# Reordering the seven products of a fast matrix multiply and giving one more of them a second level

## The chip, the cores and the metric

The kernel runs on one core of one Trainium2 chip. The metric is the device time of that core in microseconds (us), as a median over executions. A profiled execution is described by its span, from the first to the last instruction, which lies some 2 us below the time of the same run.

The engines are called as in the profile: PE is TensorE (matmul), DVE is VectorE, ACT is ScalarE, POOL is GpSimd. Each has a queue of instructions of its own.

## The reference

```python
x:  (8, 1024, 1024)   w1: (1024, 4096)   w2: (4096, 1024)      # all float32

h = x @ w1
h = 0.5 * h * (1 + np.tanh(np.sqrt(2 / np.pi) * (h + 0.044715 * h ** 3)))
return (h @ w2).astype(np.float32)
```

## The kernel before

The kernel works in fp16 with fp32 accumulation, in eight *superblocks* of 1024 rows, numbered 0 to 7. Both matmuls use a scheme of the Strassen-Winograd kind: each matrix is cut into 2 x 2 blocks, and seven products M1 to M7 of sums of blocks replace eight. Superblocks 0 and 1 use a separate routine, which also prepares and stores the sums of `w2`. The change is about `matmul2`, the second matmul of superblocks 2 to 7.

Each product multiplies a sum of blocks of the left matrix by a sum of blocks of the right one:

```python
A_TERMS = {1: ("11", "22"), 2: ("21", "22"), 3: ("11", None), 4: ("22", None),
           5: ("12", "11"), 6: ("21", "11"), 7: ("12", "22")}     # left: first minus second
INNER = (6, 7)                     # products of matmul2 that use a second level
ORDER = (4, 5, 1, 2, 3, 7, 6)      # order of the inner products
```

A *plain* product is four row blocks, each 16 matmuls of 512 columns (64 in all). DVE makes the left operand `gc` of a row block by one subtraction. A *two-level* product applies the same scheme again: seven *inner products* of 16 matmuls of 256 columns, 112 in all. DVE first makes four *inner differences* (`inner_x`), then for five of the seven inner products an *inner sum* of two of them:

```python
    def inner_x(m, g):                       # four DVE subtractions, g -> x[b]
        ...
            tt(x[b], g[u][at], g[v][at], SUB)

    def inner_product(m, x, acc, done=lambda b, t: None):
        ...                                  # seven loads of prepared sums of w2
        def product(j, bank, first):
            u, v = A_TERMS[j]
            if v is None:
                t = x[u]                     # inner products 4 and 3: no sum
            else:
                t = gcp.tile([P, HK, HT // 2], GT, name="gc")
                tt(t, x[u], x[v], SUB)       # the inner sum
            ...                              # 16 matmuls
        pb, qb, rb = psum(), psum(), psum()
        product(4, pb, True)
        v = temp()
        nc.scalar.copy(out=v, in_=pb)
        product(5, qb, True)
        u = temp()
        tt(u, v, qb, SUB)
        nc.gpsimd.tensor_tensor(out=part("11"), in0=part("11"), in1=pair(u), op=ADD)
        product(1, rb, True)
        s = temp()
        tt(s, u, rb, ADD)
        product(2, pb, False)
        s2 = temp()
        tt(s2, s, pb, SUB)
        nc.gpsimd.tensor_tensor(out=part("22"), in0=part("22"), in1=pair(s2), op=ADD)
        add("21", pb)                        # tt(part, part, bank, ADD) on DVE
        product(3, qb, False); add("12", qb)
        product(7, rb, False); add("11", rb)
        product(6, qb, False); add("22", qb)
```

The second matmul runs M4, M5, M2, M6, M3, M1, M7. Note where `x6` is made: after M4, before the loop over M5.

```python
    def matmul2(sb, g):
        ...
        for q, ps in product(4, pb, True):
            v[q] = temp()
            nc.scalar.copy(out=v[q], in_=ps)
        u2, u = halves()
        x6 = inner_x(6, g)
        for q, ps in product(5, qb, True):
            tt(u[q], v[q], ps, SUB)
        d2, d = halves()
        for q, ps in product(2, pb, False):
            ...
            tt(d[q], u[q], ps, SUB)
        inner_product(6, x6, d2)
        x7 = inner_x(7, g)
        for q, ps in product(3, qb, False):
            ...
            tt(d[q], d[q], ps, ADD)
        for q, ps in product(1, rb, True):
            tt(u[q], u[q], ps, ADD)
            tt(d[q], d[q], ps, ADD)
            store(sb, "22", q, d[q])
        ...
        inner_product(7, x7, u2)
```

`product` yields row blocks. PE's work for block q is emitted, then the body of the loop runs for it. A scheduler places the instructions of each engine; those emitted with a pin keep their order.

## Time and profile before

| | us |
|---|---|
| median of 3 runs (lowest, highest) | 1561.78 (1561.55, 1562.36) |
| profiled span | 1559.7 |
| PE busy | 1546.6 (99%) |
| mean granted PE clock | 0.998 |
| a plain product of the second matmul (64 matmuls of 512) | 13.82 |
| a two-level product, M7 (112 matmuls of 256) | 12.23 |
| the two-level product M6 | 12.52 |

Two lines of the kernel's page, the busy time of each engine and the share of each in the chain that ended last:

```profile
PE 1546.6 (99%) x7838; PEld 767.8 (49%) x7838; DVE 1004.2 (64%) x1268; ACT 473.1 (30%) x794; POOL 201.0 (13%) x292
PE 93%; DMA 3%; DVE 2%; issue 1%; SPq 1%; POOL 0%; ACT 0%; DVEq 0%
```

The kernel is bound by PE. The waits of PE (what waited, for whom, us in total, times, longest) say the same: four entries, 4.1 us in all, none in the second matmul.

```profile
PE ps L303 <- DVE u L116: 1.5, 1, 1.5
PE ps L239 <- DVE warm L719: 1.2, 1, 1.2
...
```

The timeline of PE before, superblock 4. The columns are start, duration (both us), line, output and inputs, shapes, count; a bracket at the end, where there is one, is the idle time in front and what ended it. Durations contain the pipeline's tail (the first line lasts 1.91 us, and the next starts 1.75 us after it), so products are measured from start to start.

```profile
927.67 1.91 PE L588 MATMUL ps<-u 128*128 128x256 f16 x16
929.42 5.40 PE L588 MATMUL ps<-u,gc 128*128 128x256 f16 x48
934.66 1.91 PE L588 MATMUL ps<-u 128*128 128x256 f16 x16
936.41 3.95 PE L588 MATMUL ps<-u,gc 128*128 128x256 f16 x32
940.20 13.98 PE L644 MATMUL ps<-u,g 128*128 128x512 f16 x64
954.01 13.98 PE L644 MATMUL ps<-u,gc 128*128 128x512 f16 x64
967.82 1.91 PE L588 MATMUL ps<-u 128*128 128x256 f16 x16
```

M6 is the first four lines, 927.67 to 940.20 = 12.53 us. M3 follows, then plain M1, 954.01 to 967.82 = 13.81 us. The fourth line takes 3.95 us where M7's takes 3.66: M6 loses 0.30 us there, too little for PE's waits to list.

The timeline of DVE before shows why M6 is nearly free of stalls: its four inner differences (`u<-g,g`, 4.62 us for all four) run at 887.04, beside M4, some 40 us before M6 needs them.

```profile
887.04 4.62 DVE L116 TENSOR_TENSOR u<-g,g 128x2048 f16<-128x2048 f16 x4
891.58 4.62 DVE L116 TENSOR_TENSOR gc<-g,g 128x2048 f16<-128x2048 f16 x4
```

### The profile page before, as it was taken

To read this page: it belongs to the slowest core of one execution; us is meant where nothing else is said; L and a number is where in the kernel's file an instruction comes from. 1 tells how busy PE (TensorE), PEld (TensorE's weight loads), DVE (VectorE), ACT (ScalarE), POOL (GpSimd) and SP (SyncE) were. 2 spreads that over 40 slices of the span, in tenths; PEclk is the share of its full clock that TensorE was granted. 3 is DMA by queue.
4 is the path that set the end of the run, shared out by engine and by line. 5 is a ranking of instruction groups with operands and counts; after the bars stand their busy time and mean duration, and the time that the engine had idled before them with its cause. 6 is when DMAs were issued, how large, how long until landed. Compare 5 with 4: busy or idle time off the path is not lost.

```text
span 1559.7 us, 20433 instructions
## 1 busy us (share of the span) xinstructions
PE 1546.6 (99%) x7838; PEld 767.8 (49%) x7838; DVE 1004.2 (64%) x1268; ACT 473.1 (30%) x794; POOL 201.0 (13%) x292
## 2 busy tenths in 40 slices
PE   9999999999999999999999999999999999999997
PEld 4444444444444455444554455544554445544454
DVE  6876867758755576564765647556575556655574
ACT  6644024400244103441034410343004430044210
POOL 2241012113200012000120011200111001200011
PEclk9999999999999999999999999999999999999999
DMA  9999876875984469644695446954569455663362
GB/s 317 357 324 340 252 257 221 265 231 177 342 270 132 164 251 322 194 165 149 244 355 153 186 162 239 363 147 162 186 242 334 135 189 206 235 234 135 149 237 74
DMA packets 165954, 354.73 MB, mean 227 GB/s; under 512 B 72800, under 2 KB 79968, under 8 KB 164960
## 3 DMA queue, kind: packets, MB, share of 16 engines
q1 hardware_dynamic: 147456, 282.11, 52.3%
q0 software_dynamic: 18400, 71.32, 13.9%
q8 instruction: 61, 1.00, 0.3%
q14 instruction: 37, 0.30, 0.1%
HBM read 278.92 MB, written 89.13 MB: 236 GB/s over the span
## 4 chain that ended last, share of the span: by engine, by line
PE 93%; DMA 3%; DVE 2%; issue 1%; SPq 1%; POOL 0%; ACT 0%; DVEq 0%
PE ps L303 48%; PE ps L644 39%; PE ps L588 6%; DMA gc<-in_w_dram 1%; DMA u<-w_d 1%; DVE u L116 1%; SPq L126 1%; DVE tmp L116 0%; DMA u<-in_x_dram 0%; DVE gc L116 0%; POOL u L129 0%; ACT u L153 0%; DVEq L116 0%
## 5 line engine op out<-in xcount | busy, mean ns | idle before, releaser
L303 PE MATMUL ps<-u 128*128 128x512 f16 x3584 | 776.0, 379 | 2.9 <-DVE u L116 1.5
L116 DVE TENSOR_TENSOR tmp<-tmp,ps 128x512 f32<-128x512 f32 x564 | 386.3, 686 | 309.0 <-ACT tmp L363 112.9
L303 PEld LDWEIGHTS <-u 128*128 128x128 f16 x3584 | 350.6, 98 | 426.2 <-issue 3.7
L644 PE MATMUL ps<-u,gc 128*128 128x512 f16 x1792 | 389.4, 379 | 0.0
L644 PEld LDWEIGHTS <-gc 128*128 128x128 f16 x1792 | 175.3, 98 | 211.5
L313 ACT ACTIVATE g<-tmp 128x512 f16<-128x512 f32 x256 | 161.2, 630 | 293.9 <-DVE tmp L116 293.8
L644 PE MATMUL ps<-u,g 128*128 128x512 f16 x1024 | 223.6, 379 | 0.0
L313 ACT ACTIVATE g<-ps 128x512 f16<-128x512 f32 x256 | 151.5, 596 | 90.1 <-PE ps L303 90.1
L116 DVE TENSOR_TENSOR u<-u 128x2048 f16<-128x2048 f16 (+2 forms) x154 | 159.5, 1066 | 16.1 <-ACT u L265 12.0
L397 POOL DMA_DIRECT2D out_dram<-tmp x72 | 39.5, 548 | 943.2 <-ACT tmp L688 765.1
L116 DVE TENSOR_TENSOR u<-u,ps 128x512 f32<-128x512 f32 x160 | 106.7, 682 | 83.9 <-ACT tmp L695 37.1
L644 PEld LDWEIGHTS <-g 128*128 128x128 f16 x1024 | 100.3, 98 | 119.5
L116 DVE TENSOR_TENSOR gc<-g,g 128x2048 f16<-128x2048 f16 x112 | 133.1, 1216 | 2.3 <-PE ps L644 1.6
L588 PE MATMUL ps<-u,gc 128*128 128x256 f16 x960 | 109.7, 273 | 0.8
L588 PEld LDWEIGHTS <-gc 128*128 128x128 f16 x960 | 93.9, 98 | 12.7 <-issue 1.9
L363 ACT COPY tmp<-ps 128x512 f32<-128x512 f32 x128 | 72.8, 569 | 86.5 <-PE ps L303 86.4
L116 DVE TENSOR_TENSOR gc<-u 128x2048 f16<-128x2048 f16 x60 | 73.2, 1220 | 39.2 <-PE ps L644 39.2
L116 DVE TENSOR_TENSOR tmp<-ps,tmp 128x512 f32<-128x512 f32 x128 | 88.3, 690 | 6.1 <-PE ps L303 1.2
L116 DVE TENSOR_TENSOR u<-tmp,ps 128x512 f32<-128x512 f32 x24 | 16.5, 688 | 74.7 <-PE ps L644 65.0
L688 ACT COPY tmp<-ps 128x512 f32<-128x512 f32 x24 | 14.1, 586 | 152.0 <-PE ps L644 152.0
L116 DVE TENSOR_TENSOR u<-g,g 128x2048 f16<-128x2048 f16 x48 | 59.9, 1289 | 0.0
L695 ACT COPY tmp<-ps 128x512 f32<-128x512 f32 x24 | 14.0, 585 | 133.5 <-PE ps L644 132.8
(34 smaller groups left out, 359.6 us busy)
## 6 DMA issues: line engine op xcount, KB each, us to landing
u<-w_d SPq DMA_DIRECT2D x192, 512.0 KB, 8.0
u<-raw_d SPq DMA_DIRECT2D x128, 512.0 KB, 7.3
u<-in_d SPq DMA_DIRECT2D x84, 512.0 KB, 8.7
gc<-in_w_dram SPq DMA_DIRECT2D x48, 512.0 KB, 6.0
out_dram<-tmp POOLq DMA_DIRECT2D x72, 256.0 KB, 3.2
raw_d<-u SPq DMA_DIRECT2D x32, 512.0 KB, 9.5
w_d<-u POOLq DMA_DIRECT2D x32, 512.0 KB, 4.0
xb<-in_x_dram POOLq DMA_DIRECT2D x56, 256.0 KB, 11.8
```

Of the source, the lines that this page charges most:

```text
L116: i = nc.vector.tensor_tensor(out=out, in0=in0, in1=in1, op=op)
L126: return tc.keep_in_program_order(nc.sync.dma_start(out=out, in_=in_, **kw))
L303: nc.tensor.matmul(bank, lhsT=ops[m][:, k, cs], rhs=xs[m][:, k, :], start=(first and k == 0), stop=(k == KH - 1), skip_group_check=not first,)
L313: gelu_last[0] = nc.scalar.activation(out=g[b][:, c, :], in_=src, func=GELU)
L363: nc.scalar.copy(out=v, in_=pb)
L397: return nc.gpsimd.dma_start(out=out2[r0:r0 + P, o0:o0 + OH], in_=src)
L588: nc.tensor.matmul(bank[:, i * HO:(i + 1) * HO], lhsT=t[:, c, i * P:(i + 1) * P], rhs=y[j][:, c, :], start=(first and i == 0 and c == 0), ...
L644: nc.tensor.matmul(bank, lhsT=a[:, c, :], rhs=pieces[c // QC][:, c % QC, :], start=(first and c == 0), stop=(c == NI - 1), skip_group_chec ...
L688: nc.scalar.copy(out=c21, in_=ps)
L695: nc.scalar.copy(out=c12, in_=ps)
```

## The change

The intent is to give M1 a second level in superblocks 3 to 7 (less PE work), and to free buffers for it: M1 and M4 are added into `u` first, so M4's copies no longer live in temporaries, the sums `d` come from `u` once M5 is done, and the next `x` blocks load later. The products run as M4, M1, M2, M5, M6, M3, M7. Superblock 2 keeps M1 plain and, beside it, makes and stores the sums of `w2` that a two-level M1 needs. The core of the diff, cut:

```diff
-INNER = (6, 7)
+INNER = (6, 7, 1)
...
+        p4 = product(4, pb, True)
         u2, u = halves()
-        x6 = inner_x(6, g)
+        for q, ps in p4:
+            nc.scalar.copy(out=u[q], in_=ps)
+        if sb == 2:
+            pieces = load(1)
+            for q, ps in product2(g, 1, pieces, rb, True):
+                tt(u[q], u[q], ps, ADD)
+            for j in SUMS + PLAIN:
+                split_inner(1, j, pieces)
+        else:
+            inner_product(1, inner_x(1, g), u2)
+        for q, ps in product(2, pb, False):
+            c21[q] = temp()
+            nc.scalar.copy(out=c21[q], in_=ps)
+            store(sb, "21", q, c21[q])
+        d2, d = halves()
+        xs = next_x()
         for q, ps in product(5, qb, True):
-            tt(u[q], v[q], ps, SUB)
...
-        inner_product(6, x6, d2)
-        x7 = inner_x(7, g)
+            tt(u[q], u[q], ps, SUB)
+            tt(d[q], u[q], c21[q], SUB)
+        inner_product(6, inner_x(6, g), d2)
         for q, ps in product(3, qb, False):
...
-        for q, ps in product(1, rb, True):
-            tt(u[q], u[q], ps, ADD)
-            tt(d[q], d[q], ps, ADD)
             store(sb, "22", q, d[q])
+        x7 = inner_x(7, g)
```

(The next `x` blocks are now transposed by `next_x()`, called before M5; before, they were transposed ahead of the whole second matmul.)

## The prediction

> **What bounds the kernel now.** TensorE. The page gives PE 1546.6 us of 1559.7 (99%), and the waits list of PE holds 4.1 us, all in the first 45 us. The chain of waits is 93% PE. So only matmul columns and new PE stalls can move the time.

> **What the change removes.** The PE timeline gives 13.82 us for a plain product of the second matmul (64 matmuls of 512 columns, 215.9 ns each) and 12.22 us for a two-level one (112 of 256, 109.1 ns each). [...] M1 becomes two-level in superblocks 3 to 7: 5 x 1.60 = 8.0 us less PE work. Superblock 2 keeps plain M1 and pays ten 1024-wide DVE sums (0.74 us each) and 3.7 MB of stores to prepare it; DVE has idle time there, so I count nothing.

> **What it adds and moves.** Each M1 adds four inner differences (1.29 us), five inner sums (1.22 us) and 1.7 MB more loads. Beside M4 DVE has 8 us idle, and the x transposes (16 x 1.26 us on the load queue) fall in M4 and M1, 15 us ahead of M5's loads. I see no stall at M1, M2, M3 or M7.

> **The step I expect to hurt: M6.** Before, M6's four inner differences stood in DVE's queue beside M4, long ahead. In the changed program's order they stand in M5: two after M5's third row block, then the update of u for the *fourth* block (which waits for M5's last matmul), then the third difference, the update of d, the fourth difference, and only then the sum that M6's second inner product (5) needs.  Counted from the end of M5 with the trace's start-to-start times: 0.2 (wait) + 0.6 + 1.14 + 0.6 + 1.14 + 1.22 (the sum itself) = about 5.0 us, against 1.75 us of inner product 4. PE then idles about 3.25 us, in all six superblocks 2 to 7 (the order is the same in each): 19.5 us. Before, M6 lost only 0.30 us (12.52 against 12.22), which vanishes into it: net +17.7 us.

> **Sum (an estimate from these durations):** 1561.8 - 8.0 + 17.7 = 1571.5 us, 0.6% slower. Range for 8 of 10: 1565 to 1579. Chances: faster by over 2% 0.01, within 2% 0.96, slower by over 2% 0.03.

> **What would show it.** In the PE timeline: M1 of superblocks 3 to 7 takes 12.2 to 12.5 us; M6 takes 15 to 16 us, with one gap of 3 to 3.5 us in front of its second inner product; PE's waits list names DVE (the inner sum) some 6 times, 18 to 20 us in total; all other products are unchanged. PE busy time falls by about 8 us while the span grows.

> **What would make it wrong.**
> - [...]
> - If the fourth update did not stand in the way, the time would be 1554.
> - M1 may repeat the 0.3 us stall of the old M6 (+1.5 us).

## The result, and the profile after

| | before | after |
|---|---|---|
| median, us, of the same rounds | 1562.07 (1561.55 to 1562.65, 4 runs) | 1583.15 (1582.05 to 1583.92, 4 runs) |
| profiled span, us | 1559.7 | 1580.8 |
| mean granted PE clock | 0.998 | 0.993 |

The ratio is 1.0134 (95% interval 1.0117 to 1.0152). Here and below, a ratio is the mean time of one kernel's fast runs over that of the other's of the same rounds, so it is not quite the ratio of the medians quoted. The kernel became 1.3% slower, about 21 us. The prediction was 10 us slower, and its range ended at 1579. All four runs of the changed kernel have the clock at 0.993.

The page after, the same two lines as before:

```profile
PE 1548.5 (98%) x8078; PEld 796.1 (50%) x8078; DVE 1039.1 (66%) x1294; ACT 476.2 (30%) x799; POOL 224.9 (14%) x311
PE 88%; DVE 5%; SPq 3%; DMA 2%; issue 1%; ACT 0%; DVEq 0%
```

PE has less work but is busy 1.9 us *longer*. That is the first sign that some matmuls ran slowly. The waits of PE after have two new entries, both at the two-level products:

```profile
PE ps L588 <- DVE gc L116: 19.4, 6, 3.2
PE ps L588 <- DVE u L116: 4.4, 5, 0.9
...
```

The timeline of PE after, superblock 4: two-level M1 in the first five lines, M2 and M5 in the sixth, M6 in the next four, then M3.

```profile
908.92 1.91 PE L588 MATMUL ps<-u 128*128 128x256 f16 x16
910.67 5.40 PE L588 MATMUL ps<-u,gc 128*128 128x256 f16 x48
915.91 1.91 PE L588 MATMUL ps<-u 128*128 128x256 f16 x16
917.66 1.91 PE L588 MATMUL ps<-u,gc 128*128 128x256 f16 x16
920.46 1.91 PE L588 MATMUL ps<-u,gc 128*128 128x256 f16 x16 [0.89 <-DVE u L116]
922.20 27.79 PE L644 MATMUL ps<-u,gc 128*128 128x512 f16 x128
949.83 1.91 PE L588 MATMUL ps<-u 128*128 128x256 f16 x16
954.98 6.92 PE L588 MATMUL ps<-u,gc 128*128 128x256 f16 x48 [3.24 <-DVE gc L116]
961.73 1.91 PE L588 MATMUL ps<-u 128*128 128x256 f16 x16
963.47 3.66 PE L588 MATMUL ps<-u,gc 128*128 128x256 f16 x32
966.97 13.98 PE L644 MATMUL ps<-u,g 128*128 128x512 f16 x64
```

Three things are to be read here.

1. M6 has the predicted gap before its second inner product: 3.24 us are listed, 3.25 were predicted. The two are not quite the same quantity: the prediction counted from start to start, and that delay is 954.98 - 951.58 = 3.40, since a listed idle time begins only when the pipeline has emptied (PE is still busy for 0.16 us after 951.58, in the windows below).
2. The 48 matmuls after the gap take 6.92 us. The same 48 take 5.40 in M1 above and in the kernel before. M6 as a whole lasts 966.97 - 949.83 = 17.14 us, not the 15 to 16 of the prediction.
3. M1 has a gap of its own, 0.89 listed (920.46 - 919.40 = 1.06 in truth), before its last inner product. It lasts 922.20 - 908.92 = 13.28 us, not 12.2.

The queue of DVE after, around the gap of M6. M5 ends and M6 begins on PE at 949.83; its second inner product starts after the first of the four `gc<-u` sums.

```profile
947.96 2.35 DVE L116 TENSOR_TENSOR u<-g,g 128x2048 f16<-128x2048 f16 x2
950.23 0.68 DVE L116 TENSOR_TENSOR u<-u,ps 128x512 f32<-128x512 f32 x1
950.83 1.22 DVE L116 TENSOR_TENSOR u<-g,g 128x2048 f16<-128x2048 f16 x1
951.96 0.68 DVE L116 TENSOR_TENSOR u<-u,tmp 128x512 f32<-128x512 f32 x1
952.57 1.22 DVE L116 TENSOR_TENSOR u<-g,g 128x2048 f16<-128x2048 f16 x1
953.70 4.62 DVE L116 TENSOR_TENSOR gc<-u 128x2048 f16<-128x2048 f16 x4
```

The second line is the update of `u` for M5's fourth row block. It needs M5's last matmul, and two of the four inner differences stand behind it in the same queue. This is word for word the sequence that the prediction had counted: the first sum is ready at 953.70 + 1.22 = 954.92, 5.1 us after M5's end (predicted: about 5.0; the update begins 0.40 us after M5's end and not 0.2; no idle time is listed in front of it, as the two differences ahead of it last until then).

Windows of the same place. Columns: stretch, its length, then for PE, PEld, DVE, ACT and POOL the busy time and (count), then the granted PE clock, the DMA share and GB/s.

```profile
951.58:954.98 3.40, 0.16 (x3) 0.01 (x1) 3.40 (x5) 0.58 (x1) 0.00 (x0) 0.96 0.00 0
954.98:958.08 3.10, 3.10 (x15) 2.23 (x16) 3.10 (x3) 0.00 (x0) 0.00 (x0) 0.50 0.00 0
960.00:962.00 2.00, 2.00 (x21) 1.79 (x19) 1.00 (x3) 0.00 (x0) 1.46 (x1) 1.00 0.93 352
```

The clock drops to 0.50 just before the gap ends (0.96 as the gap's mean puts the drop 0.3 us before its end) and PE then runs 3.1 us at half speed. That costs half of it, about 1.55 us, in each of the six superblocks (from the durations above, 6.92 - 5.40 = 1.52). Read in finer steps, the clock is at 0.50 from 954.68 to 958.09; such a stretch of 3.41 us is called a window from here on.

### Where the 21.1 us of the spans went

| part | predicted | measured | how measured |
|---|---|---|---|
| M6, gap | +17.7 | +18.6 | 15.62 (M6 with its gap at whole clock: 17.14 less 6.92 - 5.40) - 12.52, times 6 |
| M6, half clock | 0 | +9.1 | 102.89 (sum of the six M6 after) - 75.15 (before) - 18.6 |
| M1, superblocks 3 to 7 | -8.0 | -2.7 | (13.28 - 13.82) x 5 |
| end of the kernel, after the last product | 0 | -4.0 | 4.1 after, 8.1 before |
| start | 0 | +0.05 | the difference up to the second matmul of superblock 2 |
| sum | +9.7 | +21.1 | |

The end of the kernel is the surprise of this table. The last product ends at 1551.58 before and at 1576.72 after (start of M7 plus 12.23), and the spans end at 1559.7 and 1580.8. Between the two lies the closing work of the engines. The largest piece is the longest of POOL's three closing DRAINs, shown here before and then after (minimum / median / maximum in ns, then the first and last start):

```profile
L760 POOLq DRAIN  x3: 46/102/11681, 1547.3 to 1559.5; - x3
```

```profile
L769 POOLq DRAIN  x3: 46/102/2867, 1572.4 to 1580.5; - x3
```

The long one begins beside POOL's last addition, at 1547.3 before and 1572.4 after. Before it takes 11.68 us and ends at 1559.0, where POOL's first closing semaphore event also stands, just ahead of the span's end. After it takes 2.87 us and is over before the last product is. Nothing in the diff is meant to touch it.

### The profile page after: what moved, and what is told of

Read it like the earlier page. It is cut to its first block, busy times and chain, and to the rows that moved or that the text cites. A ratio compares the mean times of both kernels' runs of the same rounds, so it can differ in the third digit from the quotient of the medians.

```text
span 1580.8 us, 21061 instructions
## 1 busy us (share of the span) xinstructions
PE 1548.5 (98%) x8078; PEld 796.1 (50%) x8078; DVE 1039.1 (66%) x1294; ACT 476.2 (30%) x799; POOL 224.9 (14%) x311
## 4 chain that ended last, share of the span: by engine, by line
PE 88%; DVE 5%; SPq 3%; DMA 2%; issue 1%; ACT 0%; DVEq 0%
PE ps L303 47%; PE ps L644 31%; PE ps L588 10%; DVE u L116 3%; SPq L288 3%; DMA gc<-in_w_dram 1%; DVE gc L116 1%; DMA u<-in_d 1%; DVE tmp L116 1%; DMA u<-xb 1%; SPq L126 0%; ACT u L191 0%; ACT g L313 0%; SPq L577 0%; ACT u L265 0%
## 5 line engine op out<-in xcount | busy, mean ns | idle before, releaser
L644 PE MATMUL ps<-u,gc 128*128 128x512 f16 x1472 | 319.3, 379 | 0.0
L644 PEld LDWEIGHTS <-gc 128*128 128x128 f16 x1472 | 144.1, 98 | 172.6
L588 PE MATMUL ps<-u,gc 128*128 128x256 f16 x1360 | 163.9, 282 | 23.9 <-DVE gc L116 19.4
L588 PEld LDWEIGHTS <-gc 128*128 128x128 f16 x1360 | 137.1, 101 | 46.1 <-DVE gc L116 21.1
L116 DVE TENSOR_TENSOR u<-u,ps 128x512 f32<-128x512 f32 x136 | 92.6, 684 | 99.6 <-PE ps L644 52.9
L116 DVE TENSOR_TENSOR gc<-g,g 128x2048 f16<-128x2048 f16 x92 | 117.7, 1286 | 52.5 <-PE ps L644 51.1
L611 POOL TENSOR_TENSOR u<-u,tmp 128x512 f32<-128x512 f32 x17 | 37.0, 2174 | 671.2 <-DVE tmp L116 649.4
L116 DVE TENSOR_TENSOR gc<-u 128x2048 f16<-128x2048 f16 x85 | 99.8, 1219 | 0.0
L363 ACT COPY tmp<-ps 128x512 f32<-128x512 f32 x128 | 72.9, 569 | 86.7 <-PE ps L303 86.6
L116 DVE TENSOR_TENSOR u<-g,g 128x2048 f16<-128x2048 f16 x68 | 80.7, 1219 | 3.5 <-ACT g L313 3.5
L588 PE MATMUL ps<-u 128*128 128x256 f16 x544 | 64.9, 273 | 0.0
L704 ACT COPY tmp<-ps 128x512 f32<-128x512 f32 x24 | 14.1, 586 | 160.9 <-PE ps L644 160.9
## 6 DMA issues: line engine op xcount, KB each, us to landing
xb<-in_x_dram POOLq DMA_DIRECT2D x56, 256.0 KB, 11.7
```

The lines of the kernel that those rows point to most:

```text
L116: i = nc.vector.tensor_tensor(out=out, in0=in0, in1=in1, op=op)
L588: nc.tensor.matmul(bank[:, i * HO:(i + 1) * HO], lhsT=t[:, c, i * P:(i + 1) * P], rhs=y[j][:, c, :], start=(first and i == 0 and c == 0), ...
L644: nc.tensor.matmul(bank, lhsT=a[:, c, :], rhs=pieces[c // QC][:, c % QC, :], start=(first and c == 0), stop=(c == NI - 1), skip_group_chec ...
L704: nc.scalar.copy(out=c12, in_=ps)
```

## The experiments

Four theories were to be tested, each with a rival. (a) The gap of M6 comes from where the inner differences are emitted, not from M1's second level. (b) The slow matmuls after it come from the clock, which falls because of the idle time; the rival is that something else slows them, and a second question is how long a gap it takes. (c) M1's gap comes from POOL's two additions; the rivals are the number and order of DVE's operations, and the later `x` loads. (d) The shorter end comes from something that the change altered by accident. The runs came in four calls, each on one chip with the kernel before beside it (its medians 1562.07, 1562.63, 1562.27 and 1562.69), so kernels of different calls are compared through their ratios.

### e1: the inner differences of M6 made before M5's loop

Against the changed kernel:

```diff
-        for q, ps in product(5, qb, True):
+        p5 = product(5, qb, True)
+        x6 = inner_x(6, g)
+        for q, ps in p5:
...
-        inner_product(6, inner_x(6, g), d2)
+        inner_product(6, x6, d2)
```

> The changed kernel with one line moved: M6's four inner differences are made before the loop that updates u and d from M5, so in DVE's queue they stand ahead of the update that waits for M5's last matmul. Theory (queue order): the 3.24 us gap in M6 is gone in all six superblocks, with it the half clock after it; M6 takes 12.2 to 12.5 us instead of 17.1, mean clock back to 0.998, time 1583.2 - 6 x 4.7 = about 1555 us. M1's gap of 0.89 us stays. Rival (late loads: the x blocks moved to M5 or the inner operands come too late): the gap stays, about 1583 us.

Measured: 1554.07 us (1553.27 to 1554.18, 4 runs, results correct), ratio 0.9945 (0.993 to 0.996), clock 1.0. The timeline of PE at M6, superblock 4, e1:

```profile
939.76 1.91 PE L588 MATMUL ps<-u 128*128 128x256 f16 x16
941.51 5.40 PE L588 MATMUL ps<-u,gc 128*128 128x256 f16 x48
```

There is no gap, and the 48 matmuls are back at 5.40. M6 takes 12.23 us. So 29 of 1583 us hang on the position of one call. The span is 1551.2, 8.5 below the kernel before, and the same table accounts for it: M6 -0.3 x 6 = -1.8 (the old small stall is gone), M1 -2.7, the end -4.0. M1's gap of 0.89 is still there.

### e4: the new order alone, M1 plain in every superblock

Against the changed kernel:

```diff
-INNER = (6, 7, 1)
+INNER = (6, 7)
...
-        if sb == 2:
+        if True:
...
-            for j in SUMS + PLAIN:
-                split_inner(1, j, pieces)
```

> The new order of products alone, M1 one-level in every superblock, nothing stored for it. Theory: the loss is in the order, not in M1: M6 keeps its gap of 3.24 us and the half clock, 17 us in all six superblocks, M1 takes 13.8 us without a gap; 1562.6 + 27.9 = 1590 us if the end of the kernel stays as before, 1586 us if the shorter end seen after the change comes from the order. Rival (M1's second level crowds out the rest): M6 back to 12.5 us and the time near 1562.

Measured: 1592.07 us (one run, correct, state unknown), span 1590.3, clock 0.990. M6's gap is there without any second level in M1, 3.25 us in each of six places. With e1 this settles theory (a): the loss comes with the reordering, since the gap is there without M1's second level (e4), but within the new order it hangs on where M6's inner differences are emitted, since moving that one call removes it (e1).

It is 9.5 us of span slower than the changed kernel. Of these, 2.7 us are M1 (plain again) and 4.0 the end (the closing DRAIN is back at 11.687 us). The rest, 2.8 us, is nearly all clock: in two of the six places it stays at half for two windows instead of one, and the 48 matmuls take 8.13 and 8.29 us. One of them in the timeline of PE, e4:

```profile
1152.19 8.29 PE L588 MATMUL ps<-u,gc 128*128 128x256 f16 x48 [3.25 <-DVE gc L116]
```

### e2, e2b and e2c: the gap of M6 filled with matmuls of zeros

The gap keeps its cause, but PE is kept busy for a part of it by matmuls on a tile of zeros into a bank of its own. Only the clock should notice. Against the changed kernel; e2 uses 14 matmuls, e2b 4, e2c 7:

```diff
-    def inner_product(m, x, acc, done=lambda b, t: None):
+    def inner_product(m, x, acc, done=lambda b, t: None, fill=0):
...
         product(4, pb, True)
+        if fill:
+            keep_clock(psum(), fill)
...
-        inner_product(6, inner_x(6, g), d2)
+        inner_product(6, inner_x(6, g), d2, fill=14)
```

> The changed kernel with 14 matmuls on a zero tile (3.0 us) put into M6's gap, so PE waits just as long for the inner sum but is not idle. Theory (clock): no half clock after the gap, the 48 inner matmuls after it take 5.4 instead of 6.9 us, M6 takes 15.5 us instead of 17.1, mean clock 0.998, time 1583.2 - 6 x 1.55 = about 1574 us. Rival (the matmuls after the gap run slow because DVE delivers the next sums late): no change, about 1583 us. If the zero tile is too idle for the clock, also no change, but then the clock in the records stays at half.

> As the filled gap, but with only 4 zero matmuls (0.86 us) at the front of the gap, so 2.4 us of idle PE are left. If the clock falls only when nearly a whole window of 3.4 us is idle, there is no half clock here and the time is that of the fully filled gap, about 1574 us. If a shorter idle stretch suffices, M6 keeps some or all of the 1.5 us, up to 1583 us.

> As the filled gap with 7 zero matmuls: 1.7 us idle are left, half of a window of 3.41 us. Where the gap lies whole in one window and the clock still halves, half a window of idle time suffices; if the clock stays whole in all six, the limit lies between 51% and 62% of a window (the 2.4 us gaps with 62% to 70% of a window idle did halve it, the one with 38% did not).

Measured, all three correct:

| | gap listed, us | time, us | span | clock | the 48 matmuls after it |
|---|---|---|---|---|---|
| changed kernel | 3.24 | 1583.15 (4 runs) | 1580.8 | 0.993 | 6.9 to 7.0 in all six |
| e2b | 2.38 | 1582.27 (1 run, state unknown) | 1580.5 | 0.994 | 6.9 to 7.1 in five, 5.42 in one |
| e2c | 1.73 | 1580.15 (1 run, state unknown) | 1578.4 | 1.0 | 5.41 in all six |
| e2 | 0.22 | 1579.18 (1578.47 to 1579.46, 4 runs) | 1577.5 | 1.0 | 5.41 in all six |

The timeline of PE, e2, at the filled gap and at a later place of the same M6:

```profile
950.98 3.19 PE L239 MATMUL ps<-idle 128*128 128x512 f16 x14
954.38 5.41 PE L588 MATMUL ps<-u,gc 128*128 128x256 f16 x48 [0.22 <-DVE gc L116]
...
963.94 1.91 PE L588 MATMUL ps<-u,gc 128*128 128x256 f16 x16 [0.65 <-DMA u<-in_d]
```

With PE kept busy the clock stays whole (1.0, as the mean of the span), and the 48 matmuls take 5.41. That shows (b): the slow stretch comes from the idle time and not from the operands. The total is a partial miss: about 1574 was expected. M6 lasts 16.45 us instead of 17.14, where 15.6 was due. The missing 0.8 us is in the third line. The zero matmuls changed the order that the scheduler gave DVE, so that an inner difference of M7 stands ahead of an addition that the last inner product waits for. That difference takes 1.92 us instead of 1.22 and ends 1.08 us after an addition of POOL (962.21 to 963.29), as in e6 below. (The transfer named in the bracket had long landed; DVE's addition ended last, at 963.88, 0.06 us ahead of PE's start.) So filling a gap with idle work is not a neutral edit, because the scheduler answers to it. Another 0.9 us lies ahead of superblock 2's second matmul, which starts at 506.20 instead of 505.27; its cause was not looked for.

e2b tells where the limit of the clock lies, because its gaps fall on different places of a grid. In the changed kernel the clock drops at 565.56, 760.12, 954.68, 1149.24, 1343.80 and 1538.35, and rises each time 3.41 us later. The steps are 194.56 us, 57 of these stretches (194.56 / 57 = 3.413). That in these runs the edges belong to a fixed grid, and not to the gaps, shows in e4: its gaps end 195.1 to 196.5 us apart, and its drops are still 57 or 58 windows apart (194.56 or 197.97 us). Two gaps of e2b in the timeline of PE, superblocks 2 and 3:

```profile
566.35 5.42 PE L588 MATMUL ps<-u,gc 128*128 128x256 f16 x48 [2.38 <-DVE gc L116]
...
759.43 7.08 PE L588 MATMUL ps<-u,gc 128*128 128x256 f16 x48 [2.38 <-DVE gc L116]
```

The first gap has an edge of the grid in its middle, at about 565.28: 1.31 us of idle time (38% of a window) lie ahead of it, 1.07 us after it. The clock doesn't drop, and the 48 matmuls take 5.42 us. The second has the same length but lies within one window, and the clock drops 0.4 us *after* PE has resumed (the longest such delay is 0.56 us: e4, superblock 6, 1348.70 to 1349.26), as the windows of e2b show:

```profile
759.43:759.80 0.37, 0.37 (x4) 0.34 (x5) 0.37 (x1) 0.00 (x0) 0.00 (x0) 1.00 0.00 0
759.90:763.20 3.30, 3.30 (x18) 2.29 (x16) 3.30 (x4) 0.00 (x0) 0.00 (x0) 0.50 0.02 5
```

Both M6 differ in nothing else: the first lasts 576.84 - 561.20 = 15.64 us, the second 771.59 - 754.28 = 17.31. The clock costs 1.67 us, close to half of a window. In this M6 PE resumes ahead of the edge (759.43 against 759.84) and pays for the whole slow window; in the changed kernel a part of the slow window is spent waiting (954.68 to 954.98), so it costs only 1.52.

What tells the gaps with a drop from those without, in these runs, is the idle share of one window. Drops were seen at 84 to 91% (changed kernel), 62 to 70% (e2b) and 59% (e4, superblock 2: idle from 562.17, drop at 564.19, so 2.02 us). None was seen at 38% (e2b) or at 1.73 us, 51% (e2c). That e2c had at least two gaps whole within a window is an estimate: its six gaps are 193.89 us = 56.80 windows apart, so their places in the window differ by a fifth each time. A wait of e2b near its start supports it:

```profile
45.08 73.93 PE L303 MATMUL ps<-u 128*128 128x512 f16 x340 [1.73 <-DVE tmp L116]
```

### e6: M1 without POOL's two additions

Against e1, results wrong (relative error 0.65):

```diff
+        if adds:
             nc.gpsimd.tensor_tensor(out=part("11"), in0=part("11"), in1=pair(u), op=ADD)
...
+        if adds:
             nc.gpsimd.tensor_tensor(out=part("22"), in0=part("22"), in1=pair(s2), op=ADD)
...
-            inner_product(1, inner_x(1, g), u2)
+            inner_product(1, inner_x(1, g), u2, adds=False)
```

> The early-difference kernel without the two GpSimd additions in M1 (results of block 11 and 22 wrong on purpose); DVE's queue order is the same. Theory (DVE waits for GpSimd's additions): the two operand sums of M2 that stand in M1 take 1.22 us instead of 1.70 and 1.96, and M1's gap of 0.89 us before its last inner product is gone, M1 takes 12.2 to 12.3 us; time some 4 us below the early-difference kernel. Rival (the order of DVE's queue alone makes the gap): M1's gap stays at 0.5 us or more.

Measured: 1548.02 us (one run, state unknown), span 1546.2, clock 1.0. M1 takes 12.23 us and has no gap. What POOL does to DVE can be read from e1. The two operand sums of M2 that DVE makes inside M1, superblock 4, e1, timeline of DVE:

```profile
904.96 1.70 DVE L116 TENSOR_TENSOR gc<-g,g 128x2048 f16<-128x2048 f16 x1
...
907.78 1.96 DVE L116 TENSOR_TENSOR gc<-g,g 128x2048 f16<-128x2048 f16 x1
```

The two additions of POOL in the same stretch of e1:

```profile
903.40 2.18 POOL L611 TENSOR_TENSOR u<-u,tmp 128x512 f32<-128x512 f32 x1 [104.39 <-DVE tmp L116]
907.39 1.27 POOL L618 TENSOR_TENSOR u<-u,tmp 128x512 f32<-128x512 f32 x1 [1.81 <-DVE tmp L116]
```

The same two sums in e6, timeline of DVE:

```profile
904.24 1.22 DVE L116 TENSOR_TENSOR gc<-g,g 128x2048 f16<-128x2048 f16 x1
...
906.57 1.22 DVE L116 TENSOR_TENSOR gc<-g,g 128x2048 f16<-128x2048 f16 x1
```

With POOL's additions the sums take 1.70 and 1.96 us, and each ends 1.08 us after POOL's addition does (905.58 to 906.66; 908.66 to 909.74). Without them each takes 1.22. The sums look as if they did no work until POOL was through; that is a reading of these times, and what holds them up was not shown. The 1.2 us that DVE loses (0.48 and 0.74) delay the addition that frees the bank of the last inner product, and PE waits 1.06 us for it (0.89 listed), five times.

### e3: M1's two additions on DVE instead of POOL

Against e1, results correct:

```diff
-    def inner_product(m, x, acc, done=lambda b, t: None):
+    def inner_product(m, x, acc, done=lambda b, t: None, eng=None):
+        eng = eng or nc.gpsimd
...
-        nc.gpsimd.tensor_tensor(out=part("11"), in0=part("11"), in1=pair(u), op=ADD)
+        eng.tensor_tensor(out=part("11"), in0=part("11"), in1=pair(u), op=ADD)
...                                          # the same for "22"
-            inner_product(1, inner_x(1, g), u2)
+            inner_product(1, inner_x(1, g), u2, eng=nc.vector)
```

> The early-difference kernel with M1's two GpSimd additions done on DVE instead (two more additions of 0.6 us in DVE's queue, none on GpSimd). Theory (the gap in M1 comes from DVE waiting for GpSimd): operand sums back at 1.22 us, no gap, M1 12.2 to 12.3 us, about 4.4 us below the early-difference kernel, 1549 to 1550 us: faster than both kernels. Rival (DVE is simply too full in M1): the two added operations keep or lengthen the gap, 1554 us or more.

Measured: 1548.9 us (1548.13 to 1550.67, 4 runs), ratio 0.9915 (0.990 to 0.993). This is the fastest correct kernel: 13 us below the kernel before and 34 below the changed one. M1 takes 913.03 - 900.81 = 12.22 us without a gap (its last two inner products are the line below), although DVE has two more operations (0.68 us each): a longer queue with its sums at 1.22 us was quicker than a shorter one with sums of 1.70 and 1.96. The rival of (c), that DVE simply has too much to do in M1, falls with it.

```profile
909.54 3.66 PE L589 MATMUL ps<-u,gc 128*128 128x256 f16 x32
```

### e5: the next x blocks loaded early again

Against e1:

```diff
+        xs = next_x()                        # before M4
         p4 = product(4, pb, True)
...
-        xs = next_x()                        # before M5
```

> The early-difference kernel with the x blocks of the next superblock loaded before M4, as in the kernel before the change. If the later load (four buffers free for longer) is needed for M1's seven inner operands, PE waits for loads in M1 or M5, and the time rises above 1554 us. If the later load is neutral, the time stays within 2 us of the early-difference kernel.

Measured: 1554.63 us (1553.34 to 1555.88, 4 runs, correct), ratio 0.9949 (0.9933 to 0.9966), against 0.9945 for e1. M1's five gaps of 0.89 us are still there. So the later `x` loads are not their cause, and the time of the loads makes no difference that these runs can see.

### e8 and e8b: the kernel before, with more transfers issued by POOL

The closing DRAIN was long (11.68 us) in the kernel before and in e4, and short (2.1 to 2.9) in all the others. The kernels with a long one issue 230 transfers from POOL. Those with a two-level M1 store nine more pieces to prepare it and issue 239. So the kernel before was given transfers that nobody reads, 9 in e8 and 4 in e8b, in superblock 2, far from the end:

```diff
     for sb in range(NSB):
         g = matmul1(xs, sb, quads)
+        if sb == 2:
+            spare = dram.tile([P, 9, QC * HT], GT, name="spare")
+            for i in range(9):               # 4 in e8b
+                nc.gpsimd.dma_start(out=spare[:, i, :], in_=flat(g["11"][:, 0:QC, :]))
```

> The kernel before the change with nine transfers of 512 KB more, issued by GpSimd in superblock 2 to a scratch tensor that nobody reads: as many as the change adds there. Nothing else changes its place. In the four kernels with these nine transfers and in the three clock experiments GpSimd's closing drain took 2.9 us and the kernel ended 4.1 us after the last product; without them, before and with the order alone, 11.7 us and 8.1 us. Theory (the number of GpSimd's transfers sets the length of the closing drain): the end shrinks to 4.1 us, time about 1558 us, although the kernel does more. Rival (the order of the products or of the last stores sets it): still 8.1 us, 1562 us or slightly more.

> As the kernel with nine extra transfers, with four. If the drain falls with each transfer, the end lies between 4.1 and 8.1 us; if it goes in steps (some count is passed or not), it is one of the two; if the order sets it, 8.1 us.

Measured: e8 1558.9 us (1558.29 to 1559.81, 4 runs, correct), ratio 0.9975 (0.9958 to 0.9992); e8b 1557.74 (one run, correct, state unknown). POOL's closing DRAIN in e8:

```profile
L764 POOLq DRAIN  x3: 46/102/2541, 1549.7 to 1557.8; - x3
```

It is 2.54 us with 239 transfers and 2.13 us with 234 (e8b), against 11.68 with 230. After the last product e8 takes 4.0 us, as the changed kernel does. So the kernel before becomes 3.8 us faster by doing *more*: additional transfers from POOL are enough to shorten the end, and 4 do as much as 9. The -4.0 us of the table therefore comes with the added stores and not with the new order, which alone (e4) leaves the end long. Whether it is their number, their bytes or their place in superblock 2 was not separated, and what happens inside the DRAIN stays open.

## Why the prediction was wrong

- **"PE then idles about 3.25 us ... 19.5 us"** was right. The listed gap is 3.24 us, six times, in the place foretold and behind the operation foretold; e1 and e4 show that it follows from the order of emission. Reading the new queue of DVE against M5's end, with durations from the trace before, gave the delay to within 0.15 us (3.40 from start to start). That the listed 3.24 agrees to 0.01 is luck, since it leaves out the pipeline's tail, and the prediction's terms as written add up to 4.9 rather than 5.0. The cost was 18.6 net, 0.9 above the 17.7 predicted.
- **"M6 takes 15 to 16 us"** is the step that failed: it took 17.14. The prediction left the matmuls after the gap at whole clock. The clock stood only in the list of risks; what it would cost was the author's estimate, and no trace of before tested it (longest wait of PE 1.5 us, clock 0.998). Here gaps of 3.24 us brought the clock to 0.50 for 3.41 us each, and so did five of six gaps of 2.38 us, 62 to 70% of a window (e2b). Missed: +9.1 us, 1.52 per superblock. With it the time would have been 1571.5 + 9.1 = 1580.6, above the range's upper end of 1579.
- **"I see no stall at M1, M2, M3 or M7"** was right for three of them and wrong for M1: 1.06 us, five times, +5.3. The risk list had 0.3 us for it, from the old M6. There a hint stood in the trace before: two inner differences made beside an addition of POOL (933.78 us) took 2.83 us together, where 2.35 is usual. DVE's operations had been costed at the 1.22 us that they take alone; beside POOL's additions they take 1.70 and 1.96 (e1 against e6). So M1 saved 2.7 us and not 8.0.
- **The end of the kernel** didn't occur in the prediction. It gave 4.0 us back, through stores that the prediction had mentioned only as traffic. It is luck that this nearly cancels the 5.3 us of M1.
- **"PE busy time falls by about 8 us"** failed with the clock: it rose by 1.9, since matmuls at half clock are busy for longer (48 of them 6.92 us instead of 5.40). At whole clock it came true: PE is busy for 1538.3 us in e1, 8.3 less than before.
- The matmul costs held. The prediction took 109.1 ns for 256 columns and 215.9 for 512 from the trace. M1 at 12.22 us in e3 confirms the 1.60 us per product.

Put together: the predicted +9.7, and 9.1 for the clock, 0.9 for the longer delay, 5.3 for M1's gap and -4.0 for the end, is +21.0, against the measured 21.1.

## What to carry to other kernels

When a reordering moves an operation behind one that needs a result of PE in the same queue, count the queue from that result on: it foretold this delay to within 0.15 us, and hoisting one call won 29 us back. Then, in a kernel like this one, treat every PE gap beyond about half a window of 3.41 us (1.73 us brought no drop of the clock, 2.02 us did) as costing its own length and up to 1.7 us more for each slow window, and don't trust an operation's lone duration on VectorE where GpSimd works beside it (1.22 us alone, 1.70 and 1.96 beside); giving the two small additions to the "busier" engine won 5 us. Before crediting a few us to a change, look at what lies after the last useful instruction, because it can move for unrelated reasons (4.0 us here).
